# Hybrid mixer: another order of two products, a gated input that leaves its bank by two engines, and an earlier first tap

## The chip, the core and the metric

The kernel runs on one core of a Trainium2 chip. The metric is the device time in microseconds of one execution; the median of three runs is given. A core has a matrix engine (TensorE, PE in the profile), a vector engine (DVE), a scalar engine (ACT), a third elementwise engine (POOL) and a queue of its own for transfers (SP). Each engine takes its instructions in the order in which they stand in its queue; semaphores hold an instruction back until what it reads is there and what it overwrites has been read. Matrix products land in PSUM, which has eight banks here of 128 partitions by 512 numbers.

## The reference

The model has two layers with 256 tokens of 1024 numbers; every layer is a feed-forward part, a mixer and a second feed-forward part. The mixer of the first layer is the hybrid one, the only part that the change touches:

```python
def conv_ssd_mixer(u, w_in, ...):
    proj = u @ w_in
    conv_in, z, xbc, dt_raw = jnp.split(proj, [s0, s1, s2], axis=-1)
    ya = conformer_conv(conv_in, ...)          # val, gate = split(conv_in)
    yb = mamba2_ssd(z, xbc, dt_raw, ...)
    return jnp.concatenate([ya, yb], axis=-1) @ w_out

def conformer_conv(u, w_dw, b_dw, ln_g, ln_b):
    val, gate = jnp.split(u, 2, axis=-1)
    hid = causal_depthwise_conv(val * jax.nn.sigmoid(gate), w_dw, b_dw)   # 31 taps
    return jax.nn.silu(layer_norm(hid, ln_g, ln_b))
```

In `mamba2_ssd` the columns `xbc` go through a short convolution of 4 taps and a SiLU, `dt_raw` gives step sizes by a softplus, and a chunked state-space sum follows (chunks of 128 tokens, 16 heads).

## The kernel before

The 256 tokens are two tiles `t` of 128. Weights come in units of 128x2048 numbers by DMA into `raw`; each unit is split into a rounded part `wh` (copied by ACT in four pieces of 128x512) and the rest `wl` (subtracted by DVE, for units 38 to 54 by POOL). Each product is made of three passes on TensorE: high by high, high by low, low by high. The weight copies are written with `moved(LATE)`, 800 ranks later than where they stand in the program.

`Kernel` does not issue its operations as it writes them. It records them, with their operands, and a planner then puts each engine's operations in a row: each operation has a rank (its place in the program plus the offset of the `moved(...)` around it), operations whose operands are ready by the planner's costs are taken by rank, and tiles get their slots and PSUM banks as they are taken. So one offset or one line in another place changes the rows of several engines. All instructions are issued in one helper and carry its line, L466; they are told apart by the names of their tiles. PSUM is shared out by kinds (`PS_BUFS`): four banks `a`, two `w`, one `t` and one `c`.

The hybrid mixer runs from about 196 to 345 us of the span. Its steps in the order of the code:

- `gated_tok` (line 764): the first half of the 31-tap convolution's input, in two blocks `c` of 256 channels for both token tiles. `product(t, c)` makes 128 tokens by 512 columns (256 values, 256 gates) in a bank of kind `w`, and `gate_mul` follows: ACT takes a sigmoid (`sg<-w`), DVE multiplies (`pt<-sg,w`). The order is (0,0), (0,1), then (1,0) and (1,1). Per block TensorE transposes both tiles' results into bank `t` (c = 0) or `c` (c = 1): `t<-ident,pt` and `c<-ident,pt`. `consume` (line 903) then copies that bank to `cv` by ACT, 128x512 at once.
- `step_sizes`: the product with `wdt` (16 columns), a bias on DVE (`pt<-w,dtb`), small transposes, and the softplus.
- `gated_feat` twice: the second half of the convolution's input, straight in the transposed form.
- `long_conv` (line 913): the convolution in two halves `j0`, each on banks `t` and `c`. Per half, ACT sets up the four accumulators with the first tap and the bias (128x255 and 128x1 each: `t<-cv,chan` and `t<-chan`, the same with `c`) under `moved(CONV_INIT[half])`; DVE then adds 29 taps in place (`t<-cv,chan,t`) and writes the last to `cv` (`cv<-cv,chan,t`), under `moved(CONV[half])`, that is as work to fill gaps with.
- `xbc_pair`: per pair of blocks a product into a `w` and an `a` bank, ACT's first tap (`s<-w,chan`, `s<-a,chan`), three taps on DVE (`s<-w,chan,s`), and a SiLU on ACT (`s<-s`); transposes of the result (`a<-ident,s`) wait for that SiLU.
- `gate_z`: a 512-column product per token tile in a `w` bank, which ACT takes out to `y`; then the state-space sum, with exponentials on ACT (`s<-a`) and copies of the transposed inputs (`v<-a`).

The lines that the change touches are 40 (`CONV_INIT`), 767 to 783 (`gated_tok`) and 903 to 908 (`consume` and the call).

Of the kernel before, what the change touches and what calls it, by code (L numbers as in the profile page):

```python
# [12 lines left out]
AF = mybir.ActivationFunctionType  # L13
# [4 lines left out]
P = 128  # L18
# [3 lines left out]
NT = SEQ // P  # L22
# [9 lines left out]
HURRY = 2000  # L32
# [4 lines left out]
ON_POOL = (1, 1, 1)  # L37
CONV = (2000,1600)
GATE = 200
CONV_INIT = (-500, -100)  # L40
GPSIMD_UNITS = range(38, 55)
SB_BUFS = {"s": 18, "v": 4, "cv": 5, "pt": 4, "sg": 4, "x": 4, "y0": 2, "y1": 2}
PS_BUFS = {"a": 4, "w": 2, "t": 1, "c": 1}
# [502 lines left out]
class Kernel:  # L546
# [217 lines left out]
    def gated_tok(self, xT, func, consume, bank="tt", first=False):  # L764
        nc = self.nc
        units = [[self.unit(512), self.unit(512)] for _ in range(2)]
        prods = {}

        def product(t, c):
            ps = self.ps([P, 512])  # L770
            self.tok_major(ps, xT, t, units[c])
            prods[t, c] = self.gate_mul(ps, func)

        product(0, 0)
        if first:
            product(1, 0)
        product(0, 1)
        for c in range(2):
            if (1, c) not in prods:
                product(1, c)  # L780
            pt = self.ps([P, NT, 2, P], bank[c])
            for t in range(NT):
                for b in range(2):
                    nc.tensor.transpose(pt[:, t, b, :], prods[t, c][:, b * P : (b + 1) * P], self.ident)
            consume(c, pt.rearrange("p t b n -> p b t n"))
# [108 lines left out]
    def hybrid(self, xT, done):  # L894
        nc = self.nc
# [6 lines left out]

        def consume(c, src):
            g = self.slot([P, 2, SEQ], tag="cv")
            nc.scalar.activation(g.rearrange("p b (t n) -> p b t n", t=NT), src, AF.Copy)
            glu.append(g)

        self.gated_tok(xT, AF.Sigmoid, consume, "tc")
        dt, a = self.step_sizes(xT)
        for c in (2, 3):  # L910
            glu.append(self.gated_feat(xT, AF.Sigmoid))

        def long_conv():
            out = []
            for j0 in (0, 2):
                acc = [self.ps([P, 2, SEQ], tag) for tag in "tc"]
                part = lambda i: (acc[i % 2][:, i // 2, :], glu[j0 + i % 2][:, i // 2, :], 2 * (j0 + i % 2) + i // 2)
                tap = lambda ct, shift: chan[:, H_DW + ct * 31 + 30 - shift : H_DW + ct * 31 + 31 - shift]
                with nc.moved(CONV_INIT[j0 // 2]):
                    for i in range(4):  # L920
# [94 lines left out]
        for half in range(2):  # L1015
            px = [self.ps([P, 512], "a") for _ in range(NT)]
            for j in (2 * half, 2 * half + 1):
                xc = xbc_pair(j)
                for b in range(2):
                    for t in range(NT):  # L1020
                        c = (j % 2) * 2 + b
# [80 lines left out]
        for j in (2, 3, 0, 1):  # L1102
            ps = self.ps([P, 2, NT, P])
# [310 lines left out]
```

## Time and profile before

| | |
|---|---|
| median of 3 runs | 1092.56 us (1092.49 to 1092.84) |
| the profiled execution | 1092.99 us |
| its span in the trace | 1091.2 us |
| busy: PE, DVE, ACT, POOL | 1073.1, 765.6, 656.1, 141.5 us |
| granted TensorE clock | 0.999 of full speed |

The share of the span says which engine is full. The view by stretches gives the same for one stage. The timeline lists one engine's instructions in order, neighbours of one kind put together (x5): when they start, how long they are busy together, and in brackets how long the engine had been idle and what it waited for. Consecutive instructions overlap a little, so the distance from one start to the next is the better price of one in a row. The ends of matmuls are modelled.

### The profile page before, as it was taken

The numbers are of one execution on the slowest core, as the hardware profiler recorded it, in microseconds if no ns is written. First come the engines' busy times: TensorE is split into PE (matmuls) and PEld (weight loads), VectorE is DVE, ScalarE is ACT, GpSimd is POOL, SyncE is SP. The second block draws the span as 40 slices with busy tenths as digits, with TensorE's granted clock in tenths as the row PEclk, the third lists the DMA queues.
The fourth block names the chain that finished last, engine by engine and source line by source line (L and its number), as shares of the span: only waits on it lengthen the run. The fifth ranks groups of instructions, "written<-read, shape, count | busy, mean of one in ns | idle before, by whom it ended". The sixth has DMA issues, their size and how long they took to land.

```text
span 1091.2 us, 15864 instructions
## 1 busy us (share of the span) xinstructions
PE 1073.1 (98%) x5822; PEld 904.9 (83%) x5822; DVE 765.6 (70%) x1577; ACT 656.1 (60%) x1444; POOL 141.5 (13%) x136
## 2 busy tenths in 40 slices
PE   6999999999999999999999999999999999999997
PEld 5888888888878888888888888888888778888886
DVE  6756565889999885666677666668688768566563
ACT  7655555687676664655565545556576656465452
POOL 0000000169896000000000000000000400000000
PEclk9999999999999999999999999999999999999999
DMA  9755555445324575546537465554645235554621
GB/s 346 252 199 185 193 193 193 154 156 194 117 84 148 193 256 207 192 158 222 176 138 273 159 223 177 174 193 147 248 163 185 92 116 204 202 193 160 226 79 39
DMA packets 30206, 196.58 MB, mean 180 GB/s; under 512 B 3632, under 2 KB 4528, under 8 KB 7600
## 3 DMA queue, kind: packets, MB, share of 16 engines
q1 hardware_dynamic: 30128, 195.57, 51.1%
q8 instruction: 45, 0.74, 0.3%
q14 instruction: 33, 0.27, 0.1%
HBM read 194.51 MB, written 1.05 MB: 179 GB/s over the span
## 4 chain that ended last, share of the span: by engine, by line
PE 93%; DVE 3%; ACT 2%; DMA 1%; issue 0%; SPq 0%; DVEq 0%; POOLq 0%; POOL 0%; ACTq 0%
PE w L466 38%; PE a L466 32%; PE t L466 12%; PE c L466 12%; DVE c L466 1%; DVE t L466 1%; ACT wh L466 1%; DMA gain<-in_chan 1%; DVE s L466 0%; ACT junk L466 0%; SPq L466 0%; ACT c L466 0%; ACT t L466 0%; ACT s L466 0%; DVE m L466 0%
## 5 line engine op out<-in xcount | busy, mean ns | idle before, releaser
L466 ACT ACTIVATE wh<-raw 128x512 fp32r<-128x512 f32 x710 | 406.1, 628 | 204.4 <-PE a L466 83.2
L466 DVE TENSOR_TENSOR wl<-raw,wh 128x512 fp32r<-128x512 f32 x642 | 412.8, 690 | 163.2 <-ACT wh L466 162.7
L466 PE MATMUL w<-x,wh 128*128 128x512 f32 (+1 forms) x864 | 266.4, 365 | 0.9 <-DVE pt L466 0.7
L466 PE MATMUL a<-wh,s 128*128 128x512 f32 x800 | 256.5, 395 | 1.1 <-ACT s L466 1.1
L466 PE MATMUL w<-x,wl 128*128 128x256 f32 x752 | 210.9, 280 | 0.0
L466 PEld LDWEIGHTS a<-wh,s 128*128 128x128 f32 x800 | 150.0, 188 | 36.9 <-ACT s L466 2.0
L466 PEld LDWEIGHTS w<-x,wh 128*128 128x128 f32 x864 | 154.6, 188 | 28.4 <-DVE pt L466 1.0
L466 PE MATMUL w<-wh,x 128*128 128x512 f32 x512 | 169.4, 405 | 2.2 <-ACT x L466 2.1
L466 PE MATMUL a<-wl,s 128*128 128x512 f32 x400 | 157.7, 394 | 0.0
L466 PEld LDWEIGHTS w<-x,wl 128*128 128x128 f32 x752 | 142.9, 190 | 2.1 <-issue 0.9
L466 POOL TENSOR_TENSOR m<-m,mhalf 128x1 f32<-128x1 f32 x28 | 18.1, 647 | 820.9 <-DVE m L466 820.8
L466 PE MATMUL t<-x,wh 128*128 128x512 f32 x336 | 118.5, 392 | 0.0
L466 PE MATMUL c<-x,wh 128*128 128x512 f32 x336 | 118.4, 392 | 0.0
L466 PEld LDWEIGHTS w<-wh,x 128*128 128x128 f32 x512 | 96.4, 190 | 24.5 <-ACT x L466 2.8
L466 PE MATMUL w<-wl,x 128*128 128x512 f32 x256 | 102.9, 404 | 0.0
L466 PE MATMUL t<-x,wl 128*128 128x256 f32 x336 | 94.0, 280 | 0.0
L466 PE MATMUL c<-x,wl 128*128 128x256 f32 x336 | 93.9, 280 | 0.0
L466 POOL TENSOR_TENSOR wl<-raw,wh 128x512 fp32r<-128x512 f32 x68 | 85.6, 1305 | 23.9 <-ACT wh L466 23.7
L466 PEld LDWEIGHTS a<-wl,s 128*128 128x128 f32 x400 | 75.1, 188 | 16.2
L466 ACT ACTIVATE sg<-w 128x256 f32<-128x256 f32 x96 | 36.7, 383 | 80.9 <-PE w L466 80.9
L466 DVE TENSOR_TENSOR sg<-w,sg 128x256 f32<-128x256 f32 x72 | 30.5, 424 | 78.0 <-ACT sg L466 75.4
L466 PEld LDWEIGHTS c<-x,wh 128*128 128x128 f32 x336 | 63.1, 188 | 13.5
(174 smaller groups left out, 1208.4 us busy)
## 6 DMA issues: line engine op xcount, KB each, us to landing
raw<-in_weights SPq DMA_DIRECT2D x176, 1024.0 KB, 4.8
g<-in_gains SPq DMA_DIRECT2D x11, 512.0 KB, 5.4
raw<-in_weights SPq DMA_DIRECT2D x4, 256.0 KB, 6.0
raw<-in_weights SPq DMA_DIRECT2D x2, 512.0 KB, 7.8
out<-h SPq DMA_DIRECT2D x4, 256.0 KB, 2.0
g<-in_consts SPq DMA_DIRECT2D x3, 192.0 KB, 2.3
h<-in_x SPq DMA_DIRECT2D x2, 256.0 KB, 2.7
h<-in_x SPq DMA_DIRECT2D x1, 512.0 KB, 6.6
```

The costliest lines, as they stand in the source:

```text
L466: o.ins = f(*[real(a) for a in o.args], **{k: real(a) for k, a in o.kw.items()})
```

## The change

Three things, all for the hybrid mixer. `gated_tok` gets a third setting, `first=None`: product (1,0) is written ahead of product (0,1) (the feed-forward parts pass `True` or `False` and stay as they are), and product (0,1) goes to a bank of kind `a`, since three products are open at a time. `consume` is written 2000 ranks earlier, ahead of the weight copies; for c = 0 ACT copies one half of the bank and DVE the other, for c = 1 ACT copies it all. `CONV_INIT` for the first half goes from −500 to −2500.

```diff
--- before.py
+++ after.py
@@ -37,7 +37,7 @@
 ON_POOL = (1, 1, 1)
 CONV = (2000,1600)
 GATE = 200
-CONV_INIT = (-500, -100)
+CONV_INIT = (-2500, -100)
 GPSIMD_UNITS = range(38, 55)
 SB_BUFS = {"s": 18, "v": 4, "cv": 5, "pt": 4, "sg": 4, "x": 4, "y0": 2, "y1": 2}
 PS_BUFS = {"a": 4, "w": 2, "t": 1, "c": 1}
@@ -767,12 +767,12 @@
         prods = {}
 
         def product(t, c):
-            ps = self.ps([P, 512])
+            ps = self.ps([P, 512], "a" if first is None and (t, c) == (0, 1) else "w")
             self.tok_major(ps, xT, t, units[c])
             prods[t, c] = self.gate_mul(ps, func)
 
         product(0, 0)
-        if first:
+        if first is not False:
             product(1, 0)
         product(0, 1)
         for c in range(2):
@@ -902,10 +902,16 @@
 
         def consume(c, src):
             g = self.slot([P, 2, SEQ], tag="cv")
-            nc.scalar.activation(g.rearrange("p b (t n) -> p b t n", t=NT), src, AF.Copy)
+            to = g.rearrange("p b (t n) -> p b t n", t=NT)
+            with nc.moved(-HURRY):
+                if c:
+                    nc.scalar.activation(to, src, AF.Copy)
+                else:
+                    nc.scalar.activation(to[:, 0], src[:, 0], AF.Copy)
+                    nc.vector.tensor_copy(out=to[:, 1], in_=src[:, 1])
             glu.append(g)
 
-        self.gated_tok(xT, AF.Sigmoid, consume, "tc")
+        self.gated_tok(xT, AF.Sigmoid, consume, "tc", None)
         dt, a = self.step_sizes(xT)
         for c in (2, 3):
             glu.append(self.gated_feat(xT, AF.Sigmoid))
```

On ACT, where the gated products end (about 214 to 224 us in the trace of before): `sg_41` is the sigmoid of product (0,1) in before, of (1,0) in the changed kernel, `sg_42` that of the other, `sg_43` that of (1,1); `t_16` is the accumulator bank. Before:

```order
L466 ACTIVATE sg_41_2018<-w_23_1944 128x256
L466 ACTIVATE wh_37_2028<-raw_37_1763 128x512 x4
L466 ACTIVATE wh_38_2051<-raw_38_1899 128x512
L466 ACTIVATE sg_42_2059<-w_24_2000 128x256
L466 ACTIVATE wh_38_2051<-raw_38_1899 128x512 x3
L466 ACTIVATE cv_9_2078<-t_15_2049 128x512
L466 ACTIVATE t_16_2083<-cv_9_2078,chan_0_167 128x255
L466 ACTIVATE t_16_2083<-chan_0_167 128x1
L466 ACTIVATE t_16_2083<-cv_9_2078,chan_0_167 128x255
L466 ACTIVATE t_16_2083<-chan_0_167 128x1
L466 ACTIVATE wh_39_2094<-raw_39_1966 128x512 x4
L466 ACTIVATE sg_43_2120<-w_25_2054 128x256
```

and in the changed kernel:

```order
L466 ACTIVATE wh_37_2016<-raw_37_1763 128x512 x4
L466 ACTIVATE wh_38_2038<-raw_38_1899 128x512
L466 ACTIVATE sg_41_2044<-w_23_1989 128x256
L466 ACTIVATE wh_38_2038<-raw_38_1899 128x512 x3
L466 ACTIVATE cv_9_2067<-t_15_2057 128x256
L466 ACTIVATE sg_42_2070<-a_4_1944 128x256
L466 ACTIVATE t_16_2079<-cv_9_2067,chan_0_167 128x255
L466 ACTIVATE t_16_2079<-chan_0_167 128x1
L466 ACTIVATE t_16_2079<-cv_9_2067,chan_0_167 128x255
L466 ACTIVATE t_16_2079<-chan_0_167 128x1
L466 ACTIVATE wh_39_2094<-raw_39_1966 128x512 x4
L466 ACTIVATE wh_40_2122<-raw_40_2012 128x512
```

The copies `wh_37` no longer stand behind a sigmoid, `cv_9` is copied in a half, and one piece of `wh_40` stands where `sg_43` stood, which is the next row.

On DVE, the same place: `pt_7` is the gated product (1,1), `pt_8` the step sizes with their bias. Before:

```order
L466 TENSOR_TENSOR pt_6_2066<-sg_42_2059,w_24_2000 128x256
L466 SCALAR_TENSOR_TENSOR t_16_2083<-cv_9_2078,chan_0_167,t_16_2083 128x254 x2
L466 SCALAR_TENSOR_TENSOR t_16_2083<-cv_9_2078,chan_0_167,t_16_2083 128x253 x2
L466 SCALAR_TENSOR_TENSOR t_16_2083<-cv_9_2078,chan_0_167,t_16_2083 128x252
L466 TENSOR_TENSOR pt_7_2129<-sg_43_2120,w_25_2054 128x256
L466 SCALAR_TENSOR_TENSOR t_16_2083<-cv_9_2078,chan_0_167,t_16_2083 128x252
L466 SCALAR_TENSOR_TENSOR t_16_2083<-cv_9_2078,chan_0_167,t_16_2083 128x251 x2
L466 SCALAR_TENSOR_TENSOR t_16_2083<-cv_9_2078,chan_0_167,t_16_2083 128x250 x2
L466 TENSOR_SCALAR pt_8_2166<-w_26_2118,dtb_0_177 16x256
L466 SCALAR_TENSOR_TENSOR t_16_2083<-cv_9_2078,chan_0_167,t_16_2083 128x249
L466 SCALAR_TENSOR_TENSOR c_14_2161<-cv_10_102,chan_0_167,c_14_2161 128x254
```

and in the changed kernel:

```order
L466 COPY cv_9_2067<-t_15_2057 128x256
L466 TENSOR_TENSOR pt_6_2075<-sg_42_2070,a_4_1944 128x256
L466 SCALAR_TENSOR_TENSOR t_16_2079<-cv_9_2067,chan_0_167,t_16_2079 128x254 x2
L466 SCALAR_TENSOR_TENSOR t_16_2079<-cv_9_2067,chan_0_167,t_16_2079 128x253 x2
L466 SCALAR_TENSOR_TENSOR t_16_2079<-cv_9_2067,chan_0_167,t_16_2079 128x252 x2
L466 SCALAR_TENSOR_TENSOR t_16_2079<-cv_9_2067,chan_0_167,t_16_2079 128x251 x2
L466 SCALAR_TENSOR_TENSOR t_16_2079<-cv_9_2067,chan_0_167,t_16_2079 128x250
L466 TENSOR_TENSOR pt_7_2142<-sg_43_2131,w_24_2064 128x256
L466 SCALAR_TENSOR_TENSOR t_16_2079<-cv_9_2067,chan_0_167,t_16_2079 128x250
L466 SCALAR_TENSOR_TENSOR t_16_2079<-cv_9_2067,chan_0_167,t_16_2079 128x249 x2
L466 SCALAR_TENSOR_TENSOR t_16_2079<-cv_9_2067,chan_0_167,t_16_2079 128x248
L466 TENSOR_SCALAR pt_8_2174<-w_25_2125,dtb_0_177 16x256
```

Nine taps in place of five stand ahead of `pt_7`, and four in place of five between it and `pt_8`; the copy of the other half of `cv_9` is new.

On ACT, where the second half of the convolution begins (about 280 to 285 us): `t_17` and `c_15` are its accumulators, `s_37` is the short convolution's step and `s_38` its SiLU. Before:

```order
L466 ACTIVATE wh_48_2899<-raw_48_2686 128x512 x2
L466 ACTIVATE s_37_106<-a_18_2859,chan_0_167 128x256
L466 ACTIVATE wh_48_2899<-raw_48_2686 128x512 x2
L466 ACTIVATE t_17_2929<-cv_11_103,chan_0_167 128x255
L466 ACTIVATE t_17_2929<-chan_0_167 128x1
L466 ACTIVATE t_17_2929<-cv_11_103,chan_0_167 128x255
L466 ACTIVATE t_17_2929<-chan_0_167 128x1
L466 ACTIVATE s_38_2945<-s_37_106 128x512
L466 ACTIVATE s_49_2950<-order_0_75,m32_6_2295 128x128
L466 ACTIVATE c_15_2960<-cv_12_104,chan_0_167 128x255
L466 ACTIVATE c_15_2960<-chan_0_167 128x1
L466 ACTIVATE c_15_2960<-cv_12_104,chan_0_167 128x255
```

and in the changed kernel:

```order
L466 ACTIVATE wh_48_2903<-raw_48_2690 128x512 x2
L466 ACTIVATE t_17_2920<-cv_11_103,chan_0_167 128x255
L466 ACTIVATE t_17_2920<-chan_0_167 128x1
L466 ACTIVATE t_17_2920<-cv_11_103,chan_0_167 128x255
L466 ACTIVATE c_15_2930<-cv_12_104,chan_0_167 128x255
L466 ACTIVATE c_15_2930<-chan_0_167 128x1
L466 ACTIVATE t_17_2920<-chan_0_167 128x1
L466 ACTIVATE c_15_2930<-cv_12_104,chan_0_167 128x255
L466 ACTIVATE c_15_2930<-chan_0_167 128x1
L466 ACTIVATE s_37_106<-a_19_2863,chan_0_167 128x256
L466 ACTIVATE wh_48_2903<-raw_48_2690 128x512 x2
L466 ACTIVATE s_38_2969<-s_37_106 128x512
```

All eight instructions that set up `t_17` and `c_15` stand ahead of `s_37`.

SP's row is the same in both. On TensorE the instructions are the same in number and differ in order, within the hybrid mixer alone: the two products change places, the second transposes `c<-ident,pt` stand behind five more matmuls of `step_sizes`, and the transposes of `s_38` behind 26 matmuls of `gate_z` in place of 17.

## Rows read from the trace of the kernel before

**Rows 1.** The page, part 1: busy time, share of the span, instructions of each engine.
```profile
PE 1073.1 (98%) x5822; PEld 904.9 (83%) x5822; DVE 765.6 (70%) x1577; ACT 656.1 (60%) x1444; POOL 141.5 (13%) x136
```

**Rows 2.** Stretches: window, its us; busy us (instructions) by engine; clock; DMA share; GB/s.
```profile
196.00:230.00 34.00, 33.04 (x174) 26.69 (x174) 26.34 (x58) 26.24 (x59) 13.28 (x12) 1.00 0.59 191
230.00:345.00 115.00, 113.94 (x752) 98.44 (x751) 111.91 (x304) 82.69 (x179) 99.36 (x83) 1.00 0.39 136
```

**Rows 3.** Timeline of TensorE, 217 to 228: start, us, instruction, xcount, idle before and releaser.
```profile
217.07 0.38 PE L466 MATMUL t<-ident,pt 128*128 128x128 f32 x2
...
218.68 0.44 PE L466 MATMUL t<-ident,pt 128*128 128x128 f32 x2
...
224.83 0.44 PE L466 MATMUL c<-ident,pt 128*128 128x128 f32 x2 [0.28 <-DVE pt L466]
...
227.68 0.38 PE L466 MATMUL w<-x,wh 128*128 128x256 f32 x1 [0.68 <-DVE pt L466]
```

**Rows 4.** Timeline of ACT, 208 to 224.
```profile
208.49 0.66 ACT L466 ACTIVATE x<-t 128x256 fp32r<-128x256 f32 x2 [1.50 <-PE t L466]
...
214.48 2.20 ACT L466 ACTIVATE wh<-raw 128x512 fp32r<-128x512 f32 x4 [1.24 <-PE w L466]
...
219.64 0.58 ACT L466 ACTIVATE cv<-t 128x512 f32<-128x512 f32 x1
220.26 0.57 ACT L466 ACTIVATE t<-cv,chan 128x255 f32<-128x255 f32 x1
...
223.87 0.36 ACT L466 ACTIVATE sg<-w 128x256 f32<-128x256 f32 x1
```

**Rows 5.** Timeline of DVE, 209 to 229.
```profile
209.18 0.76 DVE L466 TENSOR_TENSOR x<-t,x 128x256 fp32r<-128x256 f32 x2
...
221.88 2.57 DVE L466 SCALAR_TENSOR_TENSOR t<-cv,chan,t 128x254 f32<-128x254 f32 x5 [3.25 <-ACT t L466]
224.36 0.41 DVE L466 TENSOR_TENSOR pt<-sg,w 128x256 f32<-128x256 f32 x1
224.69 2.55 DVE L466 SCALAR_TENSOR_TENSOR t<-cv,chan,t 128x252 f32<-128x252 f32 x5
227.16 0.47 DVE L466 TENSOR_SCALAR pt<-w,dtb 16x256 f32<-16x256 f32 x1
...
228.31 0.49 DVE L466 SCALAR_TENSOR_TENSOR c<-cv,chan,c 128x254 f32<-128x254 f32 x1 [0.30 <-ACT c L466]
```

**Rows 6.** Timeline of TensorE, 262 to 288.
```profile
262.58 0.44 PE L466 MATMUL a<-ident,s 128*128 128x128 f32 x2 [0.30 <-ACT s L466]
263.22 0.51 PE L466 MATMUL w<-x,wh 128*128 128x256 f32 x2 [0.20 <-DVE s L466]
...
285.81 0.62 PE L466 MATMUL w<-wh,x 128*128 128x512 f32 x2
286.27 0.40 PE L466 MATMUL w<-wl,x 128*128 128x512 f32 x1
287.11 0.51 PE L466 MATMUL a<-x,wh 128*128 128x256 f32 x2 [0.44 <-ACT v L466]
```

**Rows 7.** Timeline of ACT, 280 to 285.
```profile
280.94 0.55 ACT L466 ACTIVATE s<-a,chan 128x256 f32<-128x256 f32 x1
...
282.44 0.57 ACT L466 ACTIVATE t<-cv,chan 128x255 f32<-128x255 f32 x1
...
283.95 0.62 ACT L466 ACTIVATE s<-s 128x512 f32<-128x512 f32 x1
```

**Rows 8.** Timeline of DVE, 281 to 284.
```profile
281.04 0.48 DVE L466 SCALAR_TENSOR_TENSOR cv<-cv,chan,t 128x256 f32<-128x256 f32 x1
...
283.09 0.48 DVE L466 SCALAR_TENSOR_TENSOR s<-a,chan,s 128x253 f32<-128x253 f32 x1
```

**Rows 9.** Timeline of ACT, 305 to 314.
```profile
305.44 0.58 ACT L466 ACTIVATE y<-w 128x512 f32<-128x512 f32 x1
...
311.17 2.07 ACT L466 ACTIVATE s<-a 128x512 f32<-128x512 f32 x4
```

## The prediction

> **What bounds the kernel now.** The page comes first: TensorE is busy for 98% of the span, DVE for 70%, ACT for 60% [rows 1]. A change that adds no matmul can give or take only what TensorE waits. The view by stretches says how much that is where the diff works, in the hybrid mixer from 196 to 345 us: 34.00 − 33.04 = 0.96 us idle in the first 34 us and 115.00 − 113.94 = 1.06 us in the rest, 2.02 us together [rows 2]. The timeline names the five waits behind it: 0.28 and 0.68 us for `pt` at 224.83 and 227.68 [rows 3], 0.30 and 0.20 for `s` at 262.58 and 263.22, 0.44 for `v` at 287.11 [rows 6], 1.9 us in all. An instruction that resumes is late by some tenths more in its own start: two 512-column matmuls at 285.81 take 0.46 to the next, 0.23 each, so after the one at 286.27 the next was due at 286.50; it started at 287.11, 0.61 late where the row puts down 0.44 [rows 6]. By starts the five cost about 2.5 us. That is the whole purse: 2.0 to 2.5 of 1092.56 us. About what a measurement of this kernel can tell from no change, 0.2%, is 2.2 us.
>
> The rows of ACT and DVE show what each wait hangs on. The transposes `c<-ident,pt` at 224.83 wait for the gate of product (1,1): sigmoid at 223.87, multiplication on DVE at 224.36 [rows 3 to 5]. At 227.68 TensorE waits for `pt<-w,dtb` (227.16), which stands behind ten convolution taps `t<-cv,chan,t` (five from 221.88, five from 224.69) [rows 5]. At 262 it waits for the short convolution and its SiLU, at 287.11 for ACT.
>
> **The change, part by part.**
>
> *Products in another order.* Product (1,0) comes ahead of (0,1). Up to the first transposes at 217.07 the same number of matmuls stands ahead, 36 since the last transposes of the input, so TensorE neither gains nor loses. But the first gated input's bank is now complete with those transposes, for 218.68 before [rows 3]. On ACT the weight copies that waited 1.24 us for TensorE at 214.48 [rows 4] move up as well: what they wait for ends eight matmuls sooner, 8 × 0.23 = 1.85 us.
>
> *Eviction by two engines.* Before, one ACT copy of 128x512 took 0.58 at 219.64, behind weight copies [rows 4]. Now ACT copies one half, DVE the other. Can both read the bank at once? At 209.18 DVE's `x<-t` begins just after ACT's two reads of the same bank end (208.49 + 0.66 = 209.15) [rows 4, 5]; that is one place and no proof, but it is the only row of this kind here, so I take the halves one after the other. ACT's is priced by its 128x256 read of PSUM at 223.87 (0.36 [rows 4], I take 0.38), DVE's by its read of 256 columns of PSUM at 227.16 (0.47 [rows 5]): 217.79 to 218.17 and on to 218.66. If the halves overlap, the taps can start 0.36 sooner. The Trainium skill, page "PSUM — Partial Sum Buffer", section "PSUM bank collisions raise a hardware error", says that two engines must not access one bank in the same quadrant of partitions at the same time, two reads included. By it the split cannot give these 0.36 us, and the sum stays as it is; the row at 209.18 agrees as far as one place can.
>
> *Early initialisation.* CONV_INIT moves the first half's first taps (ACT, 128x255 and 128x1 twice, from 220.26, 1.6 us [rows 4]) ahead of the weight copies. They follow both halves and one sigmoid, at 218.71 for 220.26, and DVE's chain of taps begins at 220.33 for 221.88 [rows 5]: 1.55 us sooner. That hardly reaches TensorE. The sigmoid of product (1,1) stays at 223.87, since its matmuls end when they did. Its multiplication now has nine taps ahead of it, not five. Five such taps take 2.57 us and the last of them 0.49, so one follows another by 0.52 [rows 5]: 220.33 + 8 × 0.52 + 0.39 = 224.90, for 224.36, 0.54 later. The order puts five more of the 256-column `wdt` matmuls ahead of the transposes that wait for it, at half of 0.23 each: 0.58 us of work. Net **−0.04**. `pt<-w,dtb` has four taps behind that, not five, and runs at 227.19 for 227.16; TensorE resumes at 227.70 for 227.68: 0. Bounds of the two together: −0.36 (the overlap above) and +0.5 (one tap more ahead). What is won is won on DVE: the first tap of the second bank comes at 228.07 for 228.31 [rows 5], since one weight copy less stands ahead of its initialisation on ACT, 0.24 us.
>
> *228 to 279 us.* From that tap on as many DVE instructions stand between one short-convolution step and the next as before, so the lead remains 0.24 us. Of the waits of 0.30 and 0.20 [rows 6] it takes about 0.2: **−0.2**, bounds 0 and −0.5.
>
> *279 to 288 us.* Here the new rank does harm. Four taps that came early let the first half of the convolution end sooner on DVE (`cv<-cv,chan,t` at 279.74 for 281.04 [rows 8]), both banks come free, and ACT runs all eight initialisations of the second half in one block, *ahead* of the short-convolution step `s<-a` that stood before them at 280.94. From 282.44 to 283.95 four of them took 1.5 [rows 7]; eight take 3.1. With the block from 280.84 (two weight copies precede it), the step runs from 283.95 to 284.5. DVE's three taps on it ended 2.08 after it (280.94 + 0.55 to 283.09 + 0.48 [rows 7, 8]), so at 286.6, and the SiLU takes 0.62 [rows 7]: its end moves from 284.57 to 287.2. The order gives TensorE cover, 26 instead of 17 matmuls of 0.23 ahead of the transposes of this SiLU; from 280.28 that lasts to 286.3. So there is a new wait of 1.0 us there, and one of 0.2 behind it, because `y0<-w` now leaves its bank behind the SiLU. The old wait at 287.11 is gone. By work done: at 287.87 TensorE passes where before it passed at 287.11 [rows 6] with three matmuls (0.70) less behind it, 287.81. The lead of 0.2 is lost and 0.07 more: **+0.27**. Bounds: −0.6 if the SiLU is in time, since then only the old wait goes; +1.9 if the block starts where its taps did, at 282.44.
>
> *288 to 345 us.* The eviction `y<-w` (0.58 at 305.44) moves behind the two `v<-a`, close ahead of the four exponentials at 311.17, the first of which frees a bank for TensorE [rows 9]. It can delay them by nothing to 0.58; with shorter waits elsewhere in this stretch I take **+0.1**, bounds −0.2 and +0.5.
>
> POOL's pieces of `wl` start sooner with the copies and nothing waits for them; SP's queue is unchanged, instruction for instruction.
>
> **Sum:** −0.04 − 0.2 + 0.27 + 0.1 = +0.13 us on the profiled execution, which took 1092.99 us (span 1091.2 and 1.8 around it): 1093.1. It lies 0.43 above the median of the runs, so by the median 1092.56 + 0.13 = 1092.7 us.
>
> **The rivals.**
>
> *Slower: the SiLU starves TensorE at 286.* ACT takes its queue in order, and eight initialisations stand ahead of the step that the SiLU and then TensorE wait for. My sum has the SiLU 1.0 us late. This decides the sign, beyond 0.2%, from the point at which it ends 2.1 us later still, at 289.3. With the block at 282.44 for 280.84 the price is 1.6 more: 1094.3; if the second bank, which two more steps of DVE at 0.48 must free, holds up the block's other half too, 0.5 more: 1094.8. For it: four steps over two in-order engines without slack. Against it: DVE is not idle ahead of the release, so nothing suggests the banks come late. Chance 0.13, two thirds beyond 0.2%.
>
> *Faster: the waits vanish.* If the earlier convolution takes the load off DVE around 225 and 227 and the SiLU is in time, all five waits go, 2.0 to 2.5 us: 1090.1 to 1090.6. For it: three of the five are released by DVE. Against it: the order puts more taps ahead of the first, not fewer. Chance 0.06.
>
> *Both engines read the bank at once.* The two waits at 225 and 227 shrink by 0.36: 1092.3. Against it stands the row at 209.18. Chance 0.07. By the skill's rule, named above, it would be zero.
>
> *It does not do what it says.* Something else holds ACT's half, say its place behind `wh<-raw` copies, and the taps start when they did: 0 up to 228, no lead for 262, and a block at 280 that then comes four taps later, 1.5 us: 0.27 + 1.5 + 0.1, 1094.4. The order has the copies on ACT in the new place, so this needs them to wait for weights. Chance 0.04.
>
> **How the numbers follow.** My own sum has the rest, 0.70. Within 0.2% end the sum (save for 0.01, where its terms meet at their far ends), the overlap, the fourth rival, a third of the first and a sixth of the second: 0.69 + 0.07 + 0.04 + 0.04 + 0.01 = 0.85. Faster by over 0.2% is the rest of the second, 0.05; slower the rest of the first with that 0.01, 0.09 + 0.01 = 0.10. The range holds the sum with its bounds: down by the overlap (0.36), the rest of the waits at 262 (0.3) and a SiLU that is nearly in time (0.7), 1091.3; up to the late block and the fourth rival, 1094.4.
>
> **What would show it right or wrong.** In the trace of the changed kernel: four `t<-ident,pt` together at 217.1; ACT's half of `cv<-t` near 217.8 and DVE's half behind it; the first tap near 220.3; `c<-ident,pt` near 225.4 and `w<-x,wh` at 227.7, both with a wait; shorter waits at 262; a new wait of about 1 us near 287 in `a<-ident,s`, released by ACT's SiLU. If that SiLU ends before 286.3 or after 289, the step on the block is wrong; if DVE's half begins beside ACT's, the step on the eviction. The forecast is wrong if TensorE's idle time from 196 to 345 us moves from 2.0 us by more than 2 either way.

## The result

The changed kernel takes 1093.68 us (median of 22 runs, 1092.58 to 1095.25); the kernel before, run beside it, 1092.45 us (median of 22, 1091.36 to 1093.23). The ratio is 1.0013, with a 95% interval from 1.0007 to 1.0019: slower by 0.13%, or about 1.2 to 1.4 us, less than the 0.2% that the forecast counted as a change, but its interval excludes zero. The forecast was 1092.7 and the range 1091.3 to 1094.4.

The spans of the two profiled executions, 1091.2 and 1091.7 us, understate this, because the one of before began with a longer wait for its first operands. Three rows of TensorE in each show that (start, us, instruction, idle before it and releaser): one of its first products, and the transposes of `y` that begin the hybrid stage and those that begin the next. Before:

```profile
10.49 0.79 PE L466 MATMUL w<-wh,x 128*128 128x512 f32 x1 [2.10 <-ACT x L466]
...
196.77 0.60 PE L466 MATMUL t<-ident,y 128*128 128x128 f32 x4
...
379.05 0.60 PE L466 MATMUL t<-ident,y 128*128 128x128 f32 x4
```

and after:

```profile
9.45 0.80 PE L466 MATMUL w<-wh,x 128*128 128x512 f32 x1 [1.19 <-ACT x L466]
...
195.91 0.60 PE L466 MATMUL t<-ident,y 128*128 128x128 f32 x4
...
379.13 0.60 PE L466 MATMUL t<-ident,y 128*128 128x128 f32 x4
```

The transposes at the head of the hybrid stage stand at 196.77 and 195.91, so the changed kernel comes in 0.86 us ahead, for a reason that has nothing to do with the change (2.10 us against 1.19 us of waiting near the start). The same transposes of the next stage stand at 379.05 and 379.13. From the one to the other it is 182.28 us before and 183.22 after: **the stage costs 0.94 us more**, and beyond it the offset grows by 0.07 us at most to the end of what I compared (900 us). This length, of one stage between two like rows, is free of the luck of the start, and the experiments below are read by it as well as by their ratios. Rows of after are to be read as about 0.86 earlier than the times in the prediction.

The page's first part of after, as [rows 1]:

```profile
PE 1073.6 (98%) x5822; PEld 905.2 (83%) x5822; DVE 766.8 (70%) x1578; ACT 654.8 (60%) x1444; POOL 141.4 (13%) x136
```

and its two stretches (window, its us, then busy us of PE, PEld, DVE, ACT, POOL with instructions, clock, DMA share and GB/s), as [rows 2]:

```profile
196.00:230.00 34.00, 33.05 (x178) 27.06 (x177) 28.32 (x63) 26.38 (x59) 16.06 (x14) 1.00 0.64 217
230.00:345.00 115.00, 113.29 (x745) 97.92 (x744) 109.55 (x297) 81.37 (x177) 96.67 (x81) 1.00 0.37 129
```

TensorE's idle time in the first stretch is 0.95 us (0.96 before); in the second 1.71 us (1.06 before). The loss is behind 230 us. TensorE in the changed kernel, as [rows 3, 6]:

```profile
216.27 0.60 PE L466 MATMUL t<-ident,pt 128*128 128x128 f32 x4
...
224.49 0.44 PE L466 MATMUL c<-ident,pt 128*128 128x128 f32 x2 [0.24 <-DVE pt L466]
...
226.81 0.38 PE L466 MATMUL w<-x,wh 128*128 128x256 f32 x1 [0.71 <-DVE pt L466]
...
256.51 0.47 PE L466 MATMUL w<-x,wh 128*128 128x256 f32 x2 [0.75 <-DVE s L466]
...
262.25 0.38 PE L466 MATMUL a<-ident,s 128*128 128x128 f32 x2
...
279.68 0.66 PE L466 MATMUL a<-ident,s 128*128 128x128 f32 x4 [0.34 <-ACT s L466]
...
286.90 0.66 PE L466 MATMUL a<-ident,s 128*128 128x128 f32 x4 [0.41 <-ACT s L466]
```

The wait of 0.75 us at 256.51 is new; the one at 262 is gone; the one at 279.68 was under 0.1 before; the one at 286.90 replaces that of 287.11. ACT, as [rows 4, 7]:

```profile
216.98 0.37 ACT L466 ACTIVATE cv<-t 128x256 f32<-128x256 f32 x1
...
217.84 0.57 ACT L466 ACTIVATE t<-cv,chan 128x255 f32<-128x255 f32 x1 [0.22 <-DVE cv L466]
...
223.01 0.36 ACT L466 ACTIVATE sg<-w 128x256 f32<-128x256 f32 x1
...
274.52 0.63 ACT L466 ACTIVATE wh<-raw 128x512 fp32r<-128x512 f32 x1 [1.88 <-issue]
...
280.69 0.57 ACT L466 ACTIVATE t<-cv,chan 128x255 f32<-128x255 f32 x1
...
283.50 0.55 ACT L466 ACTIVATE s<-a,chan 128x256 f32<-128x256 f32 x1
...
286.22 0.63 ACT L466 ACTIVATE s<-s 128x512 f32<-128x512 f32 x1 [1.13 <-DVE s L466]
```

and DVE, as [rows 5]:

```profile
217.38 0.42 DVE L466 COPY cv<-t 128x256 f32<-128x256 f32 x1 [1.41 <-ACT cv L466]
...
219.46 4.65 DVE L466 SCALAR_TENSOR_TENSOR t<-cv,chan,t 128x254 f32<-128x254 f32 x9 [1.33 <-ACT t L466]
...
224.02 0.42 DVE L466 TENSOR_TENSOR pt<-sg,w 128x256 f32<-128x256 f32 x1
...
226.29 0.47 DVE L466 TENSOR_SCALAR pt<-w,dtb 16x256 f32<-16x256 f32 x1
...
227.21 0.49 DVE L466 SCALAR_TENSOR_TENSOR c<-cv,chan,c 128x254 f32<-128x254 f32 x1
...
255.89 0.47 DVE L466 SCALAR_TENSOR_TENSOR s<-w,chan,s 128x253 f32<-128x253 f32 x1
```

Up to 228 us the program ran as forecast: less 0.86, the copy of ACT's half was due at 216.93, DVE's half at 217.3, the first tap at 219.47, the transposes at 224.51, `pt<-w,dtb` at 226.33, TensorE's restart at 226.84 and the first `c` tap at 227.21. The rows have 216.98, 217.38, 219.46, 224.49, 226.29, 226.81 and 227.21.

### The profile page after: what moved, and what is told of

It reads as the page before. It is cut to its first block, busy times and chain, and to the rows that moved or that the text cites. A ratio compares the mean times of both kernels' runs of the same rounds, so it can differ in the third digit from the quotient of the medians.

```text
span 1091.7 us, 15864 instructions
## 1 busy us (share of the span) xinstructions
PE 1073.6 (98%) x5822; PEld 905.2 (83%) x5822; DVE 766.8 (70%) x1578; ACT 654.8 (60%) x1444; POOL 141.4 (13%) x136
## 3 DMA queue, kind: packets, MB, share of 16 engines
q1 hardware_dynamic: 30128, 195.57, 51.2%
## 4 chain that ended last, share of the span: by engine, by line
PE 92%; DVE 4%; ACT 2%; DMA 0%; issue 0%; SPq 0%; POOL 0%; DVEq 0%; POOLq 0%; ACTq 0%
PE w L466 37%; PE a L466 32%; PE t L466 12%; PE c L466 12%; DVE c L466 1%; DVE t L466 1%; ACT s L466 1%; DVE s L466 1%; ACT wh L466 0%; DMA gain<-in_chan 0%; ACT junk L466 0%; SPq L466 0%; ACT t L466 0%; ACT c L466 0%; DVE m L466 0%
## 5 line engine op out<-in xcount | busy, mean ns | idle before, releaser
L466 PE MATMUL a<-wh,s 128*128 128x512 f32 x800 | 256.5, 395 | 1.1 <-ACT s L466 1.1
L466 PE MATMUL w<-wh,x 128*128 128x512 f32 x496 | 164.1, 405 | 1.3 <-ACT x L466 1.2
L466 PEld LDWEIGHTS w<-wh,x 128*128 128x128 f32 x496 | 93.4, 190 | 23.4 <-ACT x L466 1.9
L466 PE MATMUL w<-wl,x 128*128 128x512 f32 x248 | 100.0, 405 | 0.0
```

The lines of the kernel that those rows point to most:

```text
L466: o.ins = f(*[real(a) for a in o.args], **{k: real(a) for k, a in o.kw.items()})
```

## The experiments

At 256.51 TensorE waits for the short convolution: the last of its three taps on the first pair's bank is the row 255.89 + 0.47 = 256.36 above. In the built program of the kernel before, that pair's `w` product and the next pair's lie in banks 3 and 2; in the changed kernel both lie in bank 2. The planner gives a tile the bank that came free last by its own reckoning, where a bank counts as free 0.1 us (`GAP`) behind its last use. In the changed kernel it reckons DVE's last tap on bank 2 to end 0.11 us before the next product starts, so bank 2 is taken again; in the kernel before it reckons that end 0.03 us behind the start, and the other bank is taken. On the chip the tap ended at 256.36, 0.60 us behind the time at which TensorE could have started (256.51 − 0.75 = 255.76). The `a` bank of product (0,1) is not what decides this: planned with the new order but that product in a `w` bank, the two tiles share a bank too, and planned with the `a` bank in the old order they do not (plans alone, neither was run). Theory A is that this bank is the loss. Theory B is that the wait merely replaces those at 262 and that the loss is made later, by the block of initialisations.

Two other questions came up. With CONV_INIT put back to (-500, -100), the planner's rows and banks of the changed kernel are the same on all five engines, and with -2500 in the kernel before they are those of before: by the plan the third part of the change does nothing; no run tests it. And ACT's row at 274.52 shows 1.88 us of idle time that the trace puts down to nothing ("issue"); I come to it with the fifth run.

Each run lists the length of the hybrid stage between the same two rows of TensorE, `t<-ident,y`; these are the first numbers of those rows.

| run | from | to | stage, us | ratio to before, 95% |
|---|---|---|---|---|
| before | 196.77 | 379.05 | 182.28 | |
| changed | 195.91 | 379.13 | 183.22 | 1.0013 (1.0007 to 1.0019) |
| e1, one bank | 195.78 | 378.35 | 182.57 | 1.0007 (0.9998 to 1.0016) |
| e2, banks in turn | 195.54 | 378.08 | 182.54 | 1.0006 (0.9997 to 1.0014) |
| e3, order alone | 196.04 | 379.12 | 183.08 | 1.0013 (1.0004 to 1.0022) |
| e4, eviction alone | 196.80 | 379.43 | 182.63 | 1.0006 (0.9997 to 1.0015) |
| e5, e2 and one ACT copy | 196.11 | 378.48 | 182.37 | 1.0007 (0.9998 to 1.0016) |
| e6, order, banks in turn | 195.68 | 378.07 | 182.39 | 1.0006 (0.9998 to 1.0015) |
| e7, e2 and a later block | 195.36 | 377.78 | 182.42 | 1.0001 (0.9992 to 1.0010) |
| e8, before, banks in turn | 196.26 | 378.44 | 182.18 | 0.9997 (0.9988 to 1.0006) |
| e9, e4 and one ACT copy | 195.57 | 378.01 | 182.44 | 1.0000 (0.9991 to 1.0009) |
| e10, all of them | 195.72 | 378.02 | 182.30 | 0.9999 (0.9990 to 1.0008) |

The intervals are some 0.9 us wide on each side and separate few of these. The stage lengths are from one profile each; how far they can be trusted shows where the kernels are alike: counted from the head of the stage, TensorE's rows in the changed kernel and e1 agree within 0.04 us over the 34 us that I compared, and over the 150 us ahead of the stage those of all twelve kernels do.

**e1: one tile in the other bank.** All instructions of all engines stand as in the changed kernel. Every `w` tile behind that one changes places with the other bank too, so which of the later tiles share a bank stays as it was.

```diff
-                    b.slot = next(i for t, i in reversed(times) if t + GAP <= s)
+                    b.slot = times[0][1] if kind.name == "w" and kind.bufs.index(b) == 32 else next(i for t, i in reversed(times) if t + GAP <= s)
```

> The changed kernel with one tile's bank changed: w_32, the product of the second short-convolution pair, goes to the w bank that has been free longest (3) and not to that of w_31 (2). All rows of all engines stay as in the changed kernel. Theory A (the time is lost to the bank): the wait of 0.75 us on DVE at 256.5 goes, TensorE is 0.9 us ahead there, gives back 0.3 to 0.5 at 262 where the waits of before partly return, and the kernel comes out 0.4 to 0.6 us faster than the changed one, ratio to before 1.0007 to 1.0009. Theory B (the wait at 256.5 only takes the place of the waits at 262, and the loss is made at 279 to 290): the waits at 262 return in full, 0.8 us by starts, and the ratio stays at 1.0013.

The stage is 0.65 us shorter. TensorE's waits from 254 to 288 us in this run:

```profile
261.95 0.50 PE L466 MATMUL w<-x,wh 128*128 128x256 f32 x2 [0.20 <-DVE s L466]
...
278.86 0.66 PE L466 MATMUL a<-ident,s 128*128 128x128 f32 x4 [0.34 <-ACT s L466]
...
286.08 0.66 PE L466 MATMUL a<-ident,s 128*128 128x128 f32 x4 [0.41 <-ACT s L466]
```

The wait at 256 is gone and, of those of before at 262, only the 0.20 at 261.95 is back. A copy of `wh` on ACT ends at 256.36 in the changed kernel too, so it might have been the releaser; in e1 it ends no sooner (255.63 + 0.63 = 256.26), and TensorE starts the product at 255.50. The copy in the changed kernel, the copy in e1, and the product in e1:

```profile
255.73 0.63 ACT L466 ACTIVATE wh<-raw 128x512 fp32r<-128x512 f32 x1 [2.19 <-PE a L466]
...
255.63 0.63 ACT L466 ACTIVATE wh<-raw 128x512 fp32r<-128x512 f32 x1 [2.19 <-PE a L466]
...
255.50 0.40 PE L466 MATMUL w<-x,wh 128*128 128x256 f32 x2
```

Theory A holds for 0.65 of the 0.94 us. The waits at 279 and 286 are untouched (0.34 and 0.41), so 0.29 us have another cause.

**e2: the two `w` banks in turn, everywhere.**

```diff
+                    b.slot = times[0][1] if kind.name == "w" else next(i for t, i in reversed(times) if t + GAP <= s)
```

> The changed kernel with every w tile in the bank that has been free longest, so that the two banks take turns. Rows of all engines as in the changed kernel. Theory A: as in the run with w_32 alone, ratio 1.0007 to 1.0009, and if other bank waits of under 0.2 us hide in the program a little less. Theory B: 1.0013.

182.54, as e1. The turns do one thing more: TensorE resumes 0.3 us sooner behind 226 us and gives that back at 262, where its waits are 0.34 and 0.31 instead of 0.20. So e1 is the clean test of the one bank.

**e3: the products' order alone**, `consume` and CONV_INIT as before (a part of the edit, against the changed kernel).

```diff
-            with nc.moved(-HURRY):
-                if c:
...
+            nc.scalar.activation(g.rearrange("p b (t n) -> p b t n", t=NT), src, AF.Copy)
```

> Only the products' order and the a bank for product (0,1); eviction by one ACT copy behind the weight copies, CONV_INIT as before. Its w_32 also shares a bank with w_31. Theory A: it has the wait at 256.5 (0.5 to 1.0 us) and with it a ratio of 1.0008 to 1.0015. Theory B: the wait may be there, but the ratio depends on the block of initialisations at 280; with that block as in before 1.0000.

It has the wait at 256 and 0.80 of the 0.94 us:

```profile
256.68 0.47 PE L466 MATMUL w<-x,wh 128*128 128x256 f32 x2 [0.73 <-ACT wh L466]
```

The trace puts this one down to ACT's copy, which ends with DVE's last tap here (256.55 and 256.53); e6 shows that it goes with the bank. The new order is what costs, as theory A says. It also brings what I had put down to CONV_INIT: with an ACT copy of both halves (0.60 us at 217.40) the first tap comes 23.60 us into the stage, for 25.11 before and 23.55 in the changed kernel, and all eight initialisations of the second half stand in one block at 280.65.

**e4: the eviction alone.**

```diff
+            to = g.rearrange("p b (t n) -> p b t n", t=NT)
+            with nc.moved(-HURRY):
+                if c:
+                    nc.scalar.activation(to, src, AF.Copy)
+                else:
+                    nc.scalar.activation(to[:, 0], src[:, 0], AF.Copy)
+                    nc.vector.tensor_copy(out=to[:, 1], in_=src[:, 1])
```

> Only the eviction: earlier in rank and split between ACT and DVE for the first bank; products in the order of before and in w banks, so w_32 and w_31 have different banks as in before. Theory A: no wait at 256.5, ratio 0.9995 to 1.0004. Theory B: the split and the earlier convolution make the block at 280, so the ratio goes to 1.0010 or more, with a wait of 0.4 us or more for the SiLU at 287.

Alone, the split is a loss on the convolution, 0.37 and 0.42 us one after the other for one copy of 0.58: the first tap comes 25.34 us into the stage, for 25.11 before. The block at 280 does not form (four initialisations from 282.85, four from 285.37). There is no wait at 256, but 0.35 us are lost. The ratio, 1.0006, lies outside the 0.9995 to 1.0004 of theory A, with an interval that reaches into it, and TensorE waits for `v` at 287 as in before: neither theory had this. TensorE's waits in this run (engine, waiting for, us in total, times, longest):

```profile
PE w L466 <- DVE pt L466: 0.9, 1, 0.9
PE a L466 <- ACT s L466: 0.6, 2, 0.3
PE a L466 <- ACT v L466: 0.4, 1, 0.4
```

0.2 us more than before are lost at 228 (0.9 for 0.7: the same ten taps stand ahead of `pt<-w,dtb`, and they begin 0.23 us later), and the wait for ACT's `s` is 0.6 in two instead of 0.3 in one: the second is that at 279.

**e5: what makes the wait at 279.** TensorE waits there for a SiLU, and every step of ACT ahead of it is late from one row on, its first copy of `wh_47`. That copy waits for a matmul of `a<-x,wh` that ends a product. In before and in e3 the copy starts 0.36 us behind that matmul's start, in the changed kernel, e1, e2 and e4 0.64 us, and all of these have the same matmul ahead of it, the same semaphores, and the same POOL and DMA operands landed long before. What differs: with the split eviction this copy stands one place earlier in ACT's whole stream of instructions (435 instead of 436, waiting instructions counted). So one instruction was added ahead of it in e2's kernel, a copy that is written twice:

```diff
         A.activation(xr, pt, AF.Copy)
+        A.activation(xr, pt, AF.Copy)
```

> The kernel with w banks taking turns, and one small ACT copy (128x32, in step_sizes) written twice, which puts every later ACT instruction one place on in ACT's instruction stream and changes no order. It is for the 0.28 us by which ACT's first copy of wh_47 (about 274) comes later behind the matmul that it waits for (0.64 us in the changed kernel and in the runs with the split, 0.36 in before and with the order alone), a gap that the trace puts down to nothing. Theory P (the place in the instruction stream): the gap goes back to 0.36, TensorE's wait at 279 from 0.5 to 0.25, and the stage from 196.8 to 379 is 0.25 us shorter than with the turns alone, 182.3 us. Theory S (something that the split eviction does): gap 0.64 and 182.55 us as before.

The row of that copy in e2:

```profile
273.47 0.63 ACT L466 ACTIVATE wh<-raw 128x512 fp32r<-128x512 f32 x1 [1.87 <-issue]
```

and in e5:

```profile
273.75 0.63 ACT L466 ACTIVATE wh<-raw 128x512 fp32r<-128x512 f32 x1 [1.59 <-issue]
```

The idle time goes from 1.87 to 1.59 us, as in before, and TensorE's wait at 279 to under 0.1:

```profile
278.91 0.66 PE L466 MATMUL a<-ident,s 128*128 128x128 f32 x4
```

The stage is 0.17 us shorter, not 0.25, since the wait for the next SiLU grows from 0.42 to 0.47. Up to the wait at 279 TensorE's rows in e2 and e5 agree within 0.05 us, counted from the head of the stage, so nothing earlier makes the difference. Theory P holds: an added instruction made the stage shorter, by an amount that the ratios (1.0006 and 1.0007) are too coarse to show. That the place in the stream matters is shown; why is not.

**e6: order alone, banks in turn.**

> The order of the products alone, with w banks taking turns. Theory A (the bank is what the new order costs): the wait of 0.73 us at 256 goes, part of it returns at 262; the stage is 182.3 to 182.6 us in place of 183.08, ratio 1.0000 to 1.0006. Theory B: the waits at 262 return in full and the stage stays at 183.0 us, ratio 1.0012.

182.39: 0.69 us less than e3, and the wait at 256 is gone. The bank accounts for most of the 0.80 us that the order costs.

**e7: the block behind the short convolution**, on e2's kernel.

```diff
-CONV_INIT = (-2500, -100)
+CONV_INIT = (-2500, 600)
```

> w banks taking turns, and CONV_INIT of the second half from -100 to 600, so that the short convolution s_37 stands ahead of the eight initialisations again and not behind them. If the block is what makes TensorE wait for the SiLU at 287 (0.4 us idle, 0.57 by starts in the changed kernel), that wait goes to under 0.25 by starts and the stage is 0.3 us shorter than with the turns alone, 182.2 us; if another wait takes its place (for v, 0.44 at 287 in before), it stays at 182.5.

ACT's short-convolution step and SiLU in this run:

```profile
279.35 0.54 ACT L466 ACTIVATE s<-a,chan 128x256 f32<-128x256 f32 x1
...
282.37 0.62 ACT L466 ACTIVATE s<-s 128x512 f32<-128x512 f32 x1
```

and on TensorE the transposes of both SiLUs and a later wait:

```profile
278.45 0.66 PE L466 MATMUL a<-ident,s 128*128 128x128 f32 x4 [0.34 <-ACT s L466]
...
283.04 0.66 PE L466 MATMUL a<-ident,s 128*128 128x128 f32 x4
...
331.62 0.63 PE L466 MATMUL w<-ident,v 128*128 128x128 f32 x4 [0.29 <-ACT y L466]
```

The wait for this SiLU is gone (0.42 in e2), and the stage is only 0.12 us shorter: a new wait of 0.29 us for ACT's `y`, at 331.62, takes most of it back. The block costs TensorE a wait, but taking it away is worth a tenth of a microsecond.

**e8: before, banks in turn.**

> The kernel before with w banks taking turns; rows of all engines as before. In before w_32 and w_31 have different banks already, so theory A expects no wait to go at 256 and a ratio of 0.9997 to 1.0002; the changed kernel with turns gained 0.3 us at 227, and if that comes from the bank of the small products there, the stage is 182.0 us in place of 182.28.

0.10 us shorter than before, not the 0.28 that was expected, and in ratio not to be told from it: what the turns save behind 226 us is lost at 262 here too.

**e9: e4 with the copy written twice**, the second trial of the place in the stream.

> The eviction alone (products in the order of before) with the small ACT copy written twice, so that all later ACT instructions stand one place on. Theory P (the place in ACT's instruction stream makes the 0.28 us at 274): the gap behind the last matmul goes from 0.64 to 0.36, TensorE's wait at 279 from 0.50 to 0.25 by starts, the stage from 182.63 to 182.36 us. Theory S (the split makes it): 182.63 us and 0.64 stay.

182.44 for 182.63, and the wait at 279 back at its old size: 0.19 us, nearly what e5 gave.

**e10: banks in turn, later block, one copy twice.**

> The changed kernel with all that the runs found: w banks taking turns, the short convolution ahead of the second block of initialisations, the small ACT copy twice. If the three add up, the stage is 182.42 - 0.18 = 182.24 us, the same as before (182.28), and the ratio to before 1.0000 within 0.0005; if one of them only moves its wait to a later place, 182.4.

182.30, what before has (182.18 with the turns, e8). With its three faults mended, the change is worth nothing either way. None of these versions beats the kernel before by more than the runs can tell.

## Why the prediction was right, and where it was wrong

The forecast of no change beyond 0.2% held, and for its main reason: the idle time of the stage, some 2 us, bounds what can be won, and what moved was waits of under a microsecond. Its size (+0.13 us) did not hold; the stage lost 0.94. What it left out, worth some 0.7 and 0.3 us at their places (below), stayed inside 0.2% by luck: nothing in the working bounds it.

*Up to 228 us* (−0.04): right, step by step, to 0.07 us, and −0.01 at TensorE's restart (30.90 us into the stage for 30.91). The halves of the eviction went one after the other: ACT's ended at 216.98 + 0.37 = 217.35 and DVE's began at 217.38. The Trainium skill's page "PSUM — Partial Sum Buffer", section "PSUM bank collisions raise a hardware error", asks software to keep two engines apart by semaphores on a bank and its quadrant. The trace agrees: DVE's copy was released by ACT's (1.41 us idle, `ACT cv`); what would happen without it, no run here shows.

*The early initialisation*: right in its times, wrong in its cause. I put the 1.55 us down to CONV_INIT. The planner's rows are the same with −500, and e3 has 1.51 of it by the order alone; the split adds 0.05 on top and, alone, takes 0.23 away (e4). The number in the diff that looked strongest was inert.

*228 to 279 us* (−0.2): **this step failed.** It counted DVE's instructions and held everything else equal. TensorE's rows were equal too, but not the banks their tiles lay in: the planner reckoned DVE to be done with a bank, and a product that was to overwrite it stood at 256.5 waiting for DVE to finish reading. The rows of an engine's order name tiles, not banks. Three rows of TensorE in before, two in the changed kernel and one in e1 show what that did:

```profile
264.29 0.39 PE L466 MATMUL a<-m,order 128*128 128x16 f32 x2
...
269.75 1.98 PE L466 MATMUL a<-s,order 128*128 128x512 f32 x4
...
279.86 0.65 PE L466 MATMUL a<-ident,s 128*128 128x128 f32 x4
```

```profile
263.42 0.32 PE L466 MATMUL a<-m,order 128*128 128x16 f32 x2
...
269.30 1.98 PE L466 MATMUL a<-s,order 128*128 128x512 f32 x4
```

```profile
268.47 1.98 PE L466 MATMUL a<-s,order 128*128 128x512 f32 x4
```

Counted from the head of the stage, the changed kernel is level with before at 263 (−0.01; the wait at 256 has taken the place of those at 262, as theory B had it), 0.41 us behind at 269, after delays of 0.15 us and less, and 0.68 behind at 279.68. In e1 TensorE is 0.29 us *ahead* of before at 269. So the lead that the step forecast was there, and of about its size; the bank, which the step left out, took 0.70 us at this place and 0.65 by the end of the stage.

*279 to 288 us* (+0.27): the mechanism came true, the size did not. All eight initialisations stand in one block (280.69 to 283.50) ahead of `s<-a` at 283.50; the SiLU follows at 286.22, and TensorE waits for it at 286.90. I had 1.0 us of waiting by starts (from when a matmul was due to when it began) and 0.17 more for `y0<-w`; the row has 0.41 idle, 0.57 by starts, and `y<-w` made no wait. TensorE came later than I had it, since it had lost time at 256 and 279, and the SiLU with it by less. By e7 the block is worth a tenth of a microsecond. I blamed the new rank for the block as well; by e3 the order makes it.

*288 to 345 us* (+0.1): TensorE idles there for 0.08 us in all (0.01 before). From 279.68 to the end of the stage the changed kernel loses 0.26 us more, where this term and the one before had 0.37 together; by the idle times nothing is lost there, so these 0.26 us are in starts a tenth or two late, and were not settled singly.

*The wait at 279* was not in the prediction either: it rested on ACT's timing as in before, and ACT's copy came 0.28 us later for its place in the instruction stream alone. TensorE loses 0.27 us there (0.41 to 0.68 behind; in e1 the whole lead of 0.29), and 0.17 to 0.19 us of it are left at the end of the stage (e5, e9).

So of 0.94 us, 0.65 is the bank (e1), 0.17 the place in ACT's stream (e2 to e5), and the remaining 0.12 is not settled.

*The rivals.* Waits that vanish: no. Both engines at one bank at once: no. It does nothing: true of CONV_INIT alone. The slow rival named the SiLU at 286 with a price of 1.6 us and more; the loss came by a wait for a bank 30 us earlier, which no rival named.

## What to carry to other kernels

Where a planner gives out banks, compare the banks of the tiles before and after a change, not only the rows: here 0.1 us of the planner's reckoning put two neighbouring tiles into one bank, and a product waited 0.75 us for a reader that was in another bank before. Ask of every number in a diff whether the order changes without it. And read effects of a tenth of a per cent between two like rows around the stage, since a wait at the start of the program varied here by as much as the whole change.

## What was not expected of the hardware

An instruction of ACT started 0.28 us later behind the same event when it stood one place earlier in its engine's stream (idle 1.87 against 1.59 us, twelve kernels in two groups: 1.87 to 1.88 in the changed kernel, e1, e2, e4 and e7, 1.59 to 1.60 in before, e3, e5, e6, e8, e9 and e10), and writing one small copy twice ahead of it shortened the stage by 0.17 and 0.19 us. The waiting instruction just ahead of this copy ends 0.32 us behind the start of the matmul that it waits for in all twelve; the copy starts 0.32 us behind that end in the first group and 0.04 in the second. So the delay lies behind the wait, and the trace shows no releaser for it.
